# Dividing the softmax exponentials while they are split into halves, in a hybrid pooling and attention layer

## The chip, the cores and the metric

The kernel runs on one core of a Trainium2 chip. Its engines take their instructions each from a queue of its own, in the order in which the program wrote them: TensorE (PE in the profile) for matrix products, VectorE (DVE), ScalarE (ACT), GpSimd (POOL), and SyncE (SP), which here only issues DMA transfers. The metric is the device time of one execution in microseconds (us).

## The reference

One layer on a sequence of 1024 tokens of width 1024, in float32:

```python
h = rmsnorm(x, norm_pre)
pool_u, pool_gate, q, k, v, attn_gate = split(h @ w_in)       # 512, 512, 512, 128, 128, 512 columns
pool_out = pool_mixer(pool_u, pool_w, pool_scale) * silu(pool_gate)
attn_out = swa_sink_attention(q, k, v, sinks) * silu(attn_gate)
y = concat([pool_out, attn_out]) @ w_out
x = x + rmsnorm(y, norm_post)
```

The attention has 8 heads of width 64 that share 2 key and value heads. Queries are taken in blocks of 128; each query sees the 128 keys up to itself, so a block's window lies in its own block of keys and the one before. The scores get a bias that falls with the distance, and each head has a sink, a logit that counts in the softmax's sum and carries no value. The pooling branch takes trailing means over 2, 4, 8 or 16 tokens in four groups of 128 channels, subtracts the token itself, and maps each group by a 128x128 matrix.

## The kernel before

**Halves.** TensorE multiplies fp16 here. Each float32 operand is scaled by a power of two and split into a high and a low fp16 half; a product is three passes (high by high, high by low, low by high; `PASSES`). A split is two instructions: ScalarE writes the high half (`AF.Copy` with a scale), VectorE the low half (value times scale minus high half, `scalar_tensor_tensor`). The power of two comes from a bound on the operand: ScalarE sums absolute values (`abssum`, line 91), TensorE spreads the column over all partitions (`spread`, line 82), VectorE takes its maximum and the power of two (lines 73 to 87).

**Slots.** The input projection is cut in 34 slots. A slot `s` makes 128 columns for 512 tokens (`proj`, line 292): 24 matmuls into one of two PSUM tiles `acc`, emptied by ScalarE in `land_slot`. Slots 0 to 9 are the keys and queries, 10 to 17 the pooling gates, 18 to 25 the pooling inputs (`u`), 26 to 33 the attention gates. Work for other parts hangs between: `middle()` runs after the twelfth matmul of a slot, `early` after the third. From slot 5 on, attention block `n` takes two slots, an even one (s = 5 + 2n, called even in the code since s - 5 is) and an odd one:

- even slot: `score_mm(n)` on TensorE, `score_land(n)` on VectorE (mask by a copy with predicate, bias, maximum of each row as `negm`), `exps(n)` on ScalarE (line 389: eight exponentials of 128x129, one per head, each with its sum)
- odd slot: `turn(n)` and `turn_low(n)` split the exponentials into `ph`; then a DMA on SP's queue transposes `ph` to `full`
- next even slot: `mask(n)` on GpSimd makes from `full` what belongs to the own block (`own`, line 427) and to the block before (`full`, line 431)
- next odd slot, at its end: `pv_mm(n)` multiplies by the values; in the even slot after that `pv_land(n)` puts the result in `cat`

In the program before, the exponentials are split undivided, scaled by 4096. The reciprocals of the sums are laid out by GpSimd to 128x512 (`r`, line 413), turned by four TensorE transposes in `divide(n)` in the middle of the next even slot (`rb`, line 442), put in `cat` by ScalarE with the value scale `vo` (line 443), and `pv_land` multiplies the product by them on VectorE (line 465). `rb` and the product `pvo` share the one buffer of the pool `ps_pv`.

**Pooling.** The landing of a `u` slot (line 476) is taken by `pool_windows` in the slot after (lines 491 to 503); in the middle of the slot after that `pool_mm` multiplies (`mixed`, line 508), and `pool_gate` (line 513) applies the gate. `sums()` in the main loop issues the windows: ahead of the projection before slot 20 (`LATE`), behind it from there. In slots 20 to 23 ScalarE turns the gates in `cat` by Silu (line 798), with one table load in slot 20.

**Output weights.** `w_out` is read twice, in eight tiles `woraw`: once for its bound (`bound_wo`, ScalarE, one tile a slot), once to be split (`split_wo` on ScalarE, `low_wo` on VectorE). `open_late` in slot 22 gives the attention's memory to the split weights.

## Time and profile before

| | us |
|---|---|
| median of 3 runs | 342.42 |
| lowest and highest run | 341.96, 1195.05 |
| the profiled execution, its span | 341.63, 339.9 |
| TensorE busy | 322.6 (95% of the span) |
| VectorE, ScalarE, GpSimd busy | 198.3, 169.6, 66.1 |

The third run, 1195.05, stands far from the other two. A time in a row below is counted from the start of the span of the profiled execution. A row of the timeline begins with the start and the duration, both in us; "idle before" in brackets is how long the engine had stood, and what released it. The span is about 1.7 us shorter than the execution's own time.

### The profile page before, as it was taken

The page shows a single profiled execution, that of the slowest core. Times are in us where ns is not written, and L with a number is a line of the kernel's source. Part 1 is how long each engine was busy: PE and PEld are TensorE (multiplying, and loading weights), DVE is VectorE, ACT ScalarE, POOL GpSimd, SP SyncE. Part 2 cuts the span into 40 slices and gives each one's busy share as a digit, 9 for nine tenths or more (in the row PEclk, how much of TensorE's full clock was granted, in tenths as well). Part 3 has the DMA queues.
Part 4 walks back from the last instruction along what each step waited for, and adds up shares of the span by engine and source line. Part 5 has one row for each costly group of instructions (what it writes and reads, how often), then busy time and mean ns, then how long its engine had stood idle before and what let it go on. Part 6 is the DMA issues. An engine that isn't in the chain of part 4 may idle for free.

```text
span 339.9 us, 5053 instructions
## 1 busy us (share of the span) xinstructions
PE 322.6 (95%) x1913; PEld 166.8 (49%) x1913; DVE 198.3 (58%) x423; ACT 169.6 (50%) x368; POOL 66.1 (19%) x73
## 2 busy tenths in 40 slices
PE   4789999999999999999979999999999999999993
PEld 2688556545445445454434444444444444444442
DVE  4977871537697444796979678833753633310122
ACT  5867831275657675888394573326543442211011
POOL 1101303000142343132405000000000233312330
PEclk9999999999999999999999999999999999999999
DMA  8976240002437376385631690320000341133111
GB/s 279 275 212 189 70 125 0 2 15 49 123 123 183 129 188 152 85 165 117 104 78 46 215 263 20 114 73 0 2 0 0 103 147 67 61 120 123 62 64 62
DMA packets 52090, 35.73 MB, mean 105 GB/s; under 512 B 35041, under 2 KB 45793, under 8 KB 52066
## 3 DMA queue, kind: packets, MB, share of 16 engines
q1 hardware_dynamic: 52064, 35.40, 38.2%
q8 instruction: 15, 0.25, 0.3%
q14 instruction: 9, 0.07, 0.1%
q10 hardware_dynamic: 2, 0.00, 0.0%
HBM read 27.01 MB, written 4.19 MB: 92 GB/s over the span
## 4 chain that ended last, share of the span: by engine, by line
PE 60%; issue 14%; DVE 10%; POOL 8%; ACT 5%; DMA 2%; POOLq 0%; DVEq 0%; ACTq 0%
PE acc L292 41%; POOL o L641 5%; PE pv L272 3%; PE y L272 3%; ACT st L389 3%; PE tp L250 2%; PE sc L360 2%; PE pvo L455 2%; PE mixed L508 2%; PE acc L272 2%; DVE o L638 2%; DMA full<-ph 1%; DVE st L377 1%; PE gain L176 1%; POOL yf L633 1%
## 5 line engine op out<-in xcount | busy, mean ns | idle before, releaser
L292 PE MATMUL acc<-hT,whl 128*128 128x512 f16 x792 | 177.1, 379 | 0.0
L292 PEld LDWEIGHTS <-whl 128*128 128x128 f16 x792 | 76.6, 98 | 91.9 <-issue 6.9
L272 PE MATMUL y<-wo,chl 128*128 128x512 f16 (+2 forms) x408 | 83.6, 366 | 0.0
L272 PEld LDWEIGHTS <-chl 128*128 128x128 f16 x408 | 39.0, 98 | 43.5
L611 ACT ACTIVATE junk<-y 128x512 bf16<-128x512 f32 (+2 forms) x17 | 9.7, 572 | 54.9 <-PE y L272 54.9
L389 ACT ACTIVATE st<-st,negm 128x129 f32<-128x129 f32 x64 | 24.8, 390 | 12.6 <-DVE negm L382 9.5
L613 DVE SCALAR_TENSOR_TENSOR eps_of<-yss,eps_of 128x1 f32<-128x1 f32 x17 | 3.2, 186 | 45.9 <-ACT junk L611 45.9
L219 ACT ACTIVATE whl<-wraw,ws 128x1024 f16<-128x1024 f32 x18 | 20.4, 1145 | 15.9 <-DVE ws L77 12.3
L633 POOL TENSOR_TENSOR yf<-eps_of,mhalf 128x1 f32<-128x1 f32 x7 | 3.8, 549 | 115.1 <-DVE eps_of L613 115.1
L223 DVE SCALAR_TENSOR_TENSOR whl<-wraw,ws,whl 128x1024 f16<-128x1024 f32 x18 | 23.7, 1325 | 0.0
L404 DVE SCALAR_TENSOR_TENSOR ph<-st,ph 128x1024 f16<-128x1024 f32 x8 | 9.8, 1226 | 21.8 <-ACT ph L399 21.8
L641 POOL TENSOR_TENSOR o<-o,xr 128x512 f32<-128x512 f32 x14 | 17.5, 1268 | 9.1 <-DVE o L638 9.1
L91 ACT ACTIVATE whl<-wraw 128x1024 bf16<-128x1024 f32 x18 | 18.8, 1049 | 0.6 <-DMA wraw<-in_w_in_dram 0.6
L427 POOL TENSOR_SCALAR_AFFINE_SELECT own<-full 128x2048 f16<-128x2048 f16 x7 | 14.5, 2072 | 22.9 <-DMA full<-ph 22.9
L413 POOL COPY r<-sums 128x512 f32<-128x512 f32 x8 | 4.9, 610 | 67.8 <-DVE sums L411 45.8
L250 PE MATMUL tp<-ident,h 128*128 128x128 f32 x64 | 11.7, 350 | 5.9 <-DVE h L241 3.4
L95 DVE SCALAR_TENSOR_TENSOR chl<-cat,cs,chl 128x1024 f16<-128x1024 f32 x8 | 10.3, 1285 | 10.2 <-ACT chl L94 10.2
L377 DVE SCALAR_TENSOR_TENSOR st<-sc,qu,bias 128x256 f32<-128x256 f32 x32 | 15.2, 484 | 1.0
L531 ACT ACTIVATE gt<-acc,wu 128x512 f32<-128x512 f32 x8 | 5.5, 687 | 18.9 <-PE acc L292 15.4
L431 POOL TENSOR_SCALAR_AFFINE_SELECT full<-full 128x2048 f16<-128x2048 f16 x7 | 14.4, 2052 | 0.5
L94 ACT ACTIVATE chl<-cat,cs 128x1024 f16<-128x1024 f32 x8 | 9.2, 1147 | 10.0 <-DVE cs L77 10.0
L250 PEld LDWEIGHTS tp<-ident,h 128*128 128x128 f32 x64 | 9.9, 182 | 7.3 <-DVE h L241 3.8
(109 smaller groups left out, 377.0 us busy)
## 6 DMA issues: line engine op xcount, KB each, us to landing
wraw<-in_w_in_dram SPq DMA_DIRECT2D x10, 512.0 KB, 5.1
x<-in_x_dram SPq DMA_DIRECT2D x8, 512.0 KB, 5.2
wraw<-in_w_in_dram SPq DMA_DIRECT2D x16, 256.0 KB, 4.7
woraw<-in_w_out_dram SPq DMA_DIRECT2D x8, 512.0 KB, 5.6
woraw<-in_w_out_dram SPq DMA_DIRECT2D x16, 256.0 KB, 7.0
xr<-in_x_dram SPq DMA_DIRECT2D x8, 512.0 KB, 3.5
out_dram<-o SPq DMA_DIRECT2D x16, 256.0 KB, 2.0
post<-in_norm_post_dram SPq DMA_DIRECT2D x1, 512.0 KB, 4.6
```

The source lines that it names most:

```text
L91: nc.scalar.activation(junk, src, AF.Abs, accum_out=m)
L95: eng.scalar_tensor_tensor(lo, src, s, hi, op0=ALU.mult, op1=ALU.subtract)
L219: nc.scalar.activation(whl[ch][:, 0], raws[ch], AF.Copy, scale=halves[ch])
L223: nc.vector.scalar_tensor_tensor(w[:, 1], raws.pop(ch), s, w[:, 0], op0=ALU.mult, op1=ALU.subtract)
L250: nc.tensor.transpose(flips[tt][b][:, block_of(i)], h[:, block_of(4 * b + i)], ident)
L272: nc.tensor.matmul(acc, a, b, start=i == 0, stop=i == len(pairs) - 1)
L292: nc.tensor.matmul(acc, w[:, a, k, :], hT[:, b, k, half_of(half)], start=k == 0 and i == 0, stop=k == KT - 1 and i == 2,)
L377: nc.vector.scalar_tensor_tensor(st[:, hs, :P], sc[:, :, 0 if n else 1, :], qu[:, 2 * pr : 2 * pr + 1], (bias if n else bias0)[:, hs, :], ...
L389: nc.scalar.activation(st[:, h, :], st[:, h, :], AF.Exp, bias=negm[:, h : h + 1], accum_out=sums[:, h : h + 1],)
L427: nc.gpsimd.affine_select(o, f, pattern=[[0, 16], [1, P]], compare_op=ALU.is_ge, fill=0.0, base=0, channel_multiplier=-1,)
L431: nc.gpsimd.affine_select(f, f, pattern=[[0, 16], [-1, P]], compare_op=ALU.is_ge, fill=0.0, base=-1, channel_multiplier=1,)
L641: nc.gpsimd.tensor_tensor(o[:, hs], o[:, hs], xr[:, hs], op=ALU.add)
```

## The change

The reciprocal of each sum, times 4096, is made ahead of the split (`turn`), and the split takes it as its scale: eight 128x128 instructions on ScalarE and eight on VectorE, a pair for each head, in place of one 128x1024 instruction on each. The layout on GpSimd, the transposes on TensorE and `divide` go. `pv_land` becomes a copy with the value scale on ScalarE, in place of a product on VectorE. In the main loop `turn` stands behind `sums()` and `lows()` before slot 20, and in slot 20 behind the Silu and ahead of the projection. The bounds of the output weights go from slots 11 to 18 to slots 17 to 24 (`WO`), their loads with them, and the second loads and the high halves come two slots later; the last low halves come two in a slot where two are ready.

```diff
     def turn(n):
         st, sums = att_s.pop(n)
         ph = att.tile([P, 2, 8, P], F16, tag="ph", name="ph")
-        nc.scalar.activation(ph[:, 0], st[:, :, :P], AF.Copy, scale=4096.0)
+        nc.vector.tensor_scalar(sums, sums, 2.0**-12, None, op0=ALU.mult)
+        nc.vector.reciprocal(sums, sums)
+        for h in range(8):
+            nc.scalar.activation(
+                ph[:, 0, h], st[:, h, :P], AF.Copy, scale=sums[:, h : h + 1]
+            )
         att_f[n] = (st, sums, ph)
 
     def turn_low(n):
         st, sums, ph = att_f[n]
-        nc.vector.scalar_tensor_tensor(
-            ph[:, 1], st[:, :, :P], 4096.0, ph[:, 0], op0=ALU.mult, op1=ALU.subtract
-        )
+        for h in range(8):
+            nc.vector.scalar_tensor_tensor(
+                ph[:, 1, h], st[:, h, :P], sums[:, h : h + 1], ph[:, 0, h],
+                op0=ALU.mult, op1=ALU.subtract,
+            )
...
-        nc.vector.reciprocal(sums, sums)
-        r = t2.tile([P, 512], F32, tag="t2", name="r")
-        nc.gpsimd.tensor_copy(
-            r.rearrange("p (c kv d) -> p c kv d", c=4, kv=2),
-            sums.rearrange("p (kv c) -> p c kv", kv=2).unsqueeze(3).broadcast_to([P, 4, 2, HD]),
-        )
...
-    def divide(n):
-        r = att_r.pop(n)
-        rb = ps_pv.tile([P, 512], F32, tag="pv", name="rb")
-        for c in range(4):
-            nc.tensor.transpose(rb[:, block_of(c)], r[:, block_of(c)], ident)
-        nc.scalar.activation(
-            cat[:, 4:8, block_of(n)], rb.rearrange("p (c t) -> p c t", t=P), AF.Copy, scale=vo
-        )
...
     def pv_land(n):
-        dst, pv = cat[:, 4:8, block_of(n)], att_o.pop(n)
-        nc.vector.tensor_tensor(dst, pv.rearrange("p (c t) -> p c t", t=P), dst, op=ALU.mult)
+        nc.scalar.activation(
+            cat[:, 4:8, block_of(n)], att_o.pop(n).rearrange("p (c t) -> p c t", t=P),
+            AF.Copy, scale=vo,
+        )
...
+        WO = 17
...
-            elif n < NB:
-                turn(n)
...
-                if not odd and 1 <= n <= NB:
-                    divide(n - 1)
...
+            if odd and n < NB and s >= LATE:
+                turn(n)
             if s < LATE:
                 sums()
                 lows()
+                if odd and n < NB:
+                    turn(n)
                 acc = proj(ch, half, middle)
...
-                if s >= 26 and wo_lo < wo_hi:
-                    low_wo(wo_lo)
-                    wo_lo += 1
+                for _ in range(2 if s >= 31 else 1):
+                    if wo_lo < wo_hi:
+                        low_wo(wo_lo)
+                        wo_lo += 1
...
-            if 9 <= s < 9 + KT:
-                wo_raw["b", s - 9] = load_wo(s - 9)
-            if 11 <= s < 11 + KT:
-                bound_wo(s - 11)
-            if s == 11 + KT:
+            if WO - 2 <= s < WO - 2 + KT:
+                wo_raw["b", s - WO + 2] = load_wo(s - WO + 2)
+            if WO <= s < WO + KT:
+                bound_wo(s - WO)
+            if s == WO + KT - 1:
...
-            if s >= 23 and wo_hi < KT:
+            if s >= 25 and wo_hi < KT:
...
-            if 21 <= s < 21 + KT:
-                wo_raw["o", s - 21] = load_wo(s - 21)
+            if WO + KT - 2 <= s < WO + 2 * KT - 2:
+                wo_raw["o", s - WO - KT + 2] = load_wo(s - WO - KT + 2)
```

VectorE before, in block 1, from the low half of an input weight (L223) past the power of two of the next weights (L87 to L213) to the split of the exponentials (L404), the landing of a query slot (L95) and `pv_land` (L465):

```order
L223 SCALAR_TENSOR_TENSOR whl<-wraw,ws,whl 128x1024
L87 TENSOR_REDUCE amall<-spread 128x1
L73 TENSOR_SCALAR wp<-amall 128x1
L76 TENSOR_SCALAR wp<-wp 128x1
L77 RECIPROCAL ws<-wp 128x1
L213 TENSOR_TENSOR wu<-wp,gsc 128x1
L404 SCALAR_TENSOR_TENSOR ph<-st,ph 128x1024
L411 RECIPROCAL sums<-sums 128x8
L95 SCALAR_TENSOR_TENSOR qT<-acc,qT 128x512
L465 TENSOR_TENSOR cat<-pvo,cat 128x4x128
```

The same place of the changed kernel:

```order
L223 SCALAR_TENSOR_TENSOR whl<-wraw,ws,whl 128x1024
L399 TENSOR_SCALAR sums<-sums 128x8
L400 RECIPROCAL sums<-sums 128x8
L87 TENSOR_REDUCE amall<-spread 128x1
L73 TENSOR_SCALAR wp<-amall 128x1
L76 TENSOR_SCALAR wp<-wp 128x1
L77 RECIPROCAL ws<-wp 128x1
L213 TENSOR_TENSOR wu<-wp,gsc 128x1
L410 SCALAR_TENSOR_TENSOR ph<-st,sums,ph 128x128 x8
L95 SCALAR_TENSOR_TENSOR qT<-acc,qT 128x512
```

The reciprocals, which need the sums of all exponentials, now stand ahead of the power of two; `pv_land` is gone from the engine.

VectorE before, in slot 20, from the windows of the second pooling slot (L491 to L503, `u` slot 19) over the split of block 7 to the gate of the first:

```order
L491 TENSOR_TENSOR win<-ug 128x527
L491 TENSOR_TENSOR win<-win 128x525
L497 SCALAR_TENSOR_TENSOR res<-win,ug 128x512
L502 TENSOR_TENSOR win<-win,invc 128x3
L503 TENSOR_TENSOR res<-win,ug 128x3
L404 SCALAR_TENSOR_TENSOR ph<-st,ph 128x1024
L411 RECIPROCAL sums<-sums 128x8
L513 SCALAR_TENSOR_TENSOR cat<-mixed,pscale,cat 128x512
```

The same place of the changed kernel:

```order
L399 TENSOR_SCALAR sums<-sums 128x8
L400 RECIPROCAL sums<-sums 128x8
L483 TENSOR_TENSOR win<-ug 128x527
L483 TENSOR_TENSOR win<-win 128x525
L489 SCALAR_TENSOR_TENSOR res<-win,ug 128x512
L494 TENSOR_TENSOR win<-win,invc 128x3
L495 TENSOR_TENSOR res<-win,ug 128x3
L410 SCALAR_TENSOR_TENSOR ph<-st,sums,ph 128x128 x8
L505 SCALAR_TENSOR_TENSOR cat<-mixed,pscale,cat 128x512
```

The reciprocals of block 7 have come ahead of these windows.

ScalarE before, from the exponentials of block 7 (L389) to the next landings; L798 is the Silu of a gate, L476 and L481 land `u`:

```order
L389 ACTIVATE st,sums<-st,negm 128x129 x8
L399 ACTIVATE ph<-st 128x1024
L798 ACT_TABLE_LOAD
L798 ACTIVATE cat<-cat 128x1024
L476 ACTIVATE ug<-acc,wu 128x512
L481 ACTIVATE tails<-acc,wu 128x16
```

The same place of the changed kernel:

```order
L389 ACTIVATE st,sums<-st,negm 128x129 x8
L790 ACT_TABLE_LOAD
L790 ACTIVATE cat<-cat 128x1024
L402 ACTIVATE ph<-st,sums 128x128 x8
L91 ACTIVATE junk,wom<-woraw 128x1024
L468 ACTIVATE ug<-acc,wu 128x512
L473 ACTIVATE tails<-acc,wu 128x16
```

The split of block 7 now stands behind the table load and the first Silu, and the bound of an output weight tile ahead of the landing.

## Rows read from the trace of the kernel before

**Rows 1.** The page's busy times: us, share of the span, instructions.

```profile
PE 322.6 (95%) x1913; PEld 166.8 (49%) x1913; DVE 198.3 (58%) x423; ACT 169.6 (50%) x368; POOL 66.1 (19%) x73
```

**Rows 2.** Timeline of TensorE around the first three `divide`.

```profile
77.75 0.27 PE L82 MATMUL spread<-ident,as 128*128 128x128 f32 x1
77.86 0.60 PE L442 MATMUL rb<-ident,r 128*128 128x128 f32 x4
78.30 5.34 PE L292 MATMUL acc<-hT,whl 128*128 128x512 f16 x24
...
91.05 0.27 PE L82 MATMUL spread<-ident,as 128*128 128x128 f32 x1
...
92.55 5.34 PE L292 MATMUL acc<-hT,whl 128*128 128x512 f16 x24
...
103.35 2.76 PE L292 MATMUL acc<-hT,whl 128*128 128x512 f16 x12
...
106.80 7.93 PE L292 MATMUL acc<-hT,whl 128*128 128x512 f16 x36
```

**Rows 3.** Groups by line: count, busy us, mean ns, idle before.

```profile
L389 ACT ACTIVATE st<-st,negm 128x129 f32<-128x129 f32 x64 | 24.8, 390 | 12.6 <-DVE negm L382 9.5 <-POOL full L431 3.0
...
L404 DVE SCALAR_TENSOR_TENSOR ph<-st,ph 128x1024 f16<-128x1024 f32 x8 | 9.8, 1226 | 21.8 <-ACT ph L399 21.8
...
L399 ACT ACTIVATE ph<-st 128x1024 f16<-128x1024 f32 x8 | 8.5, 1057 | 0.3
...
L465 DVE TENSOR_TENSOR cat<-pvo,cat 128x512 f32<-128x512 f32 x8 | 5.3, 665 | 0.3 <-PE pvo L455 0.3
...
L613 DVE SCALAR_TENSOR_TENSOR eps_of<-yss,eps_of 128x1 f32<-128x1 f32 x17 | 3.2, 186 | 45.9 <-ACT junk L611 45.9
...
L411 DVE RECIPROCAL sums<-sums 128x8 f32<-128x8 f32 x8 | 1.6, 196 | 0.0
```

**Rows 4.** Timeline of all engines, from block 1's masks to block 2's product.

```profile
93.82 1.24 DVE L213 TENSOR_TENSOR wu<-wp,gsc 128x1 f32<-128x1 f32 x1
...
94.99 0.16 DVE L371 COPY st<-sinks 128x8 f32<-128x8 f32 x1
...
99.85 0.41 ACT L389 ACTIVATE st<-st,negm 128x129 f32<-128x129 f32 x1 [3.71 <-DVE negm L382]
...
105.46 1.65 SPq L408 DMA_TRANSPOSE full<-ph  x1
...
109.24 2.00 POOL L427 TENSOR_SCALAR_AFFINE_SELECT own<-full 128x2048 f16<-128x2048 f16 x1 [2.99 <-DMA full<-ph]
...
114.66 0.84 PE L455 MATMUL pvo<-own,vst 128*64 128x512 f16 x6
115.33 0.81 PE L455 MATMUL pvo<-full,vst 128*64 128x512 f16 x6
```

**Rows 5.** Timeline of all engines in slots 20 and 21, block 7.

```profile
168.83 0.41 ACT L389 ACTIVATE st<-st,negm 128x129 f32<-128x129 f32 x1 [3.02 <-POOL full L431]
...
169.44 0.71 DVE L491 TENSOR_TENSOR win<-ug 128x527 f32<-128x527 f32 x1
...
171.85 0.16 DVE L503 TENSOR_TENSOR res<-win,ug 128x3 f32<-128x3 f32 x1
...
172.42 2.76 PE L292 MATMUL acc<-hT,whl 128*128 128x512 f16 x12
173.13 1.28 ACT L798 ACT_TABLE_LOAD   x1
...
175.39 0.67 ACT L476 ACTIVATE ug<-acc,wu 128x512 f32<-128x512 f32 x1
...
177.49 1.02 PE L508 MATMUL mixed<-res,pw 128*128 128x512 f32 x2
```

**Rows 6.** The same timeline, where GpSimd's mask of block 7 meets VectorE.

```profile
178.36 2.48 POOL L427 TENSOR_SCALAR_AFFINE_SELECT own<-full 128x2048 f16<-128x2048 f16 x1 [3.11 <-DMA full<-ph]
...
179.01 2.37 DVE L497 SCALAR_TENSOR_TENSOR res<-win,ug 128x512 f32<-128x512 f32 x1
```

More of the change, by code (lines that the diff above doesn't have):

```diff
@@ L410, in turn_low @@
         )
-        nc.vector.reciprocal(sums, sums)
-        r = t2.tile([P, 512], F32, tag="t2", name="r")
-        nc.gpsimd.tensor_copy(
-            r.rearrange("p (c kv d) -> p c kv d", c=4, kv=2),
-            sums.rearrange("p (kv c) -> p c kv", kv=2).unsqueeze(3).broadcast_to([P, 4, 2, HD]),
-        )
         att_f[n] = full
-        att_r[n] = r
     def mask(n):
```

## The prediction

> **What bounds the kernel now.** The page's busy times come first: TensorE is busy 95% of the span, the others 58% and less [rows 1]. So an edit is worth what it takes off TensorE's own queue or out of its waits, and costs what it makes TensorE wait for. The timeline of TensorE around `divide` is read next, by starts, since ends of matmuls overlap. Twelve more matmuls in a burst take 7.93 - 5.34 = 2.59 us, 0.216 each [rows 2]. The first `divide` holds the queue for 78.30 - 77.86 = 0.44. The second, from the `spread` ahead of it, takes 92.55 - 91.05 = 1.50, against 78.30 - 77.75 = 0.55 at the first: 0.95 more, waiting for the shared buffer, so 1.39. The third takes 106.80 - 103.35 - 2.59 = 0.86. The last, in slot 21, takes 177.49 - 172.42 - 2.59 = 2.48 [rows 5]. The four between show no wait: 0.44 each. Last I followed one attention block through all engines, since TensorE meets its result two slots later: block 2 [rows 4] and block 7 [rows 5].
>
> **What is removed.** 0.44 + 1.39 + 0.86 + 4 x 0.44 + 2.48 = 6.9 us of TensorE's queue. This is the most that the change can give, 2.0% of the profiled 341.63. GpSimd loses eight layouts and VectorE eight `pv_land`, 0.67 each [rows 3]; ScalarE's copy in `pv_land` replaces that in `divide`, of the same size.
>
> **What is added to a block's chain.** From the first exponential to the DMA's issue the kernel before takes 5.61 in block 2 (99.85 to 105.46) [rows 4]. Out of it go one ScalarE copy, 1.06, and one VectorE low half, 1.23 [rows 3]. In come:
> - two small VectorE instructions on 128x8, 0.2 each by the reciprocal's row, and one more change of engine, estimated at 0.1: 0.5.
> - eight 128x128 ScalarE copies with a scale from memory. No such row exists. Lower end: an eighth of the large copy, 0.13 each, 1.06 in all; upper end: the exponential of a head, nearly the same shape and with a pointer too, 0.39 each, 3.1 in all [rows 3]. ScalarE's neighbours overlap: a table load at 173.13 of 1.28 and a Silu of the large copy's size, 1.06, would end at 175.47, and the next starts at 175.39 [rows 5]. So 8 x (0.39 - 0.08) + 0.08 = 2.5, near the upper end, because its row has the same shape.
> - eight VectorE low halves. Each runs one head behind ScalarE, so only the last counts. Between a one-column instruction, 0.186, and the large one, 1.226, in proportion to width: 0.32 [rows 3].
>
> Sum: 0.5 + 2.5 + 0.32 - 1.06 - 1.23 = +1.0 a block; the ends give -0.4 and, with no overlap of the two engines (2.6), about +3.9.
>
> **Blocks 1 and 2.** ScalarE's queue behind block 1's split (a weight's high half, a bound, the landing of a query slot) moves 0.5 + 1.44 = 1.9 later, and VectorE's low half of that landing with it. Without `pv_land` VectorE gets 0.67 back. Whether it also gets back 1.05 at L213, which took 1.24 beside GpSimd's mask where a one-column instruction takes 0.19, is open [rows 3, 4]. So `score_land(2)`, at 94.99 before, starts 0.2 to 1.2 later, and the DMA of block 2, 1.0 more, 1.2 to 2.2 later: 106.7 to 107.7. From issue to the own mask it takes 109.24 - 105.46 = 3.78, and a mask 2.0 [rows 4]. The own mask ends at 112.4 to 113.4, the other one at 114.5 to 115.5. TensorE, freed of three divides (2.69), comes to the product at 114.66 - 2.69 = 111.97 and waits for both. Its second half starts at 114.5 to 115.5; it was 115.33 [rows 4]. Of 2.7 us gained to there some 0.3 is left: **the loss is 2.4**. A stall here gives later blocks time; I see no further wait in blocks 3 to 6, whose four divides bring 1.76. TensorE leads by 2.1.
>
> **Block 7.** TensorE would end the first half of slot 21 at 172.42 + 2.59 - 2.1 = 172.9, and then wants the windows of the second `u` slot (`mixed`). Before, VectorE made them from 169.44 to 172.01, beside the exponentials of block 7, and had them done early [rows 5]. Now the reciprocals stand ahead of them and wait for all eight exponentials: queued behind are these windows, behind them TensorE. Block 6's exponentials can start some 0.7 to 1.2 earlier by the lead there, its split pushes the `u` landing behind it 1.9 later; the windows before `score_land(7)`, and so block 7's exponentials, come 0.7 to 1.2 later: 169.5 to 170.0 instead of 168.83. Eight of them take 3.1, the reciprocals 0.5, the windows 2.57: 175.7 to 176.2. **TensorE waits 3.0** and starts `mixed` at 176.0 instead of 177.49: lead 1.5. Slot 22 needs the accumulator of slot 20 back. ScalarE now has, from the exponentials' end at 172.9, table load 1.28, Silu 1.06, split 2.5, a weight bound of the moved series about 1.06 (a 1024-wide row), landing 0.9: 179.7. TensorE would be there at 176.0 + 0.86 + 2.59 = 179.45: a wait of 0.25. The third `u` slot's windows, one longer by 0.71, need 3.3 from that landing, 179.4: 182.7, against TensorE's 182.3: 0.4 more. The lead at the end is 0.8. Block 7's masks are done before its product.
>
> ScalarE's page in the Trainium skill ("ScalarE: Activation LUTs", What ACT_TABLE_LOAD costs) puts a drain of 1.38 us on every table switch besides the load. The trace disagrees: between 173.13 and 175.39 there is room for load and Silu alone [rows 5]. By the page the split of block 7 and the landing would come 1.4 later, and the sum would be a gain of nothing instead of 0.8.
>
> **The moved bounds.** Eight ScalarE instructions leave slots 11 to 18 and come in slots 17 to 24, where each stands ahead of a landing; that is in the sum above. Their loads now share SP's queue with the transposes of blocks 5 to 7: the order on the queue puts loads behind a transpose that waits for a split, with two slots between load and use as cover (over 10 us; without it ScalarE, and the landing behind, would stand). The high halves of `w_out` end two slots later, hidden since the last low half stays in slot 33, where it was. The column's `spread` only moves. Priced at nothing.
>
> **Forecast.** 6.9 - 2.4 - 3.0 - 0.25 - 0.4 = 0.8 (rounded), so 340.8 for an execution like the profiled one. That one lies 0.3 and 0.8 below the other two undisturbed runs (341.96, 342.42); their middle is 342.0, and I predict 341.2.
>
> **Rivals.**
> - *The heads are cheap.* If a ScalarE head costs nearer to 0.13 than 0.31, block 2's mask is there before TensorE, and block 7's chain starts earlier: about 2 us come back at block 2 and 1 to 1.5 at block 7, a gain of 4: 338.0. For it speaks the large copy's rate, against it the exponential's row. If the windows' wait vanished too, all 6.9 would stay: 335.1.
> - *VectorE and GpSimd collide: slower than before.* In block 7 the row of `res` takes 2.37 beside GpSimd's own mask, which runs from 178.36 for 2.48 [rows 6]; the rate of the line in row 169.44 (0.71 for about the same width) says what it takes alone. Now the masks start 3.78 after an issue near 178.1, at 181.9, and the third windows end at 182.7: the mask would catch their last instructions, which read two tiles. Then `mixed` waits up to 2.2 more, and the next mask may take another 1 to 2 from the windows of the fourth slot: 0.8 becomes a loss of 1.4 to 3.4, 343.4 to 345.4. It decides from the point at which these windows are unfinished when the mask begins. For it: the times lie within 1 us. Against: an instruction that has begun holds on, and a slightly shorter split puts the windows ahead.
> - *The drain* of the page, which the row denies: 342.0.
>
> The Trainium skill's "SBUF — State Buffer" (Who interferes with whom) has a VectorE instruction with two SBUF inputs and a GpSimd one that reads SBUF block each other fully. By that rule the collision is all or nothing; the row at 179.01 agrees, with its 2.37.
>
> **How the numbers follow.** Forecast 0.5 (339.7 to 342.5); cheap heads 0.22 (335.1 to 339.7); collision 0.22 (342.5 to 345.4); drain 0.03; the upper end of the chain at every block, above 345.4, 0.03. The range that leaves out 0.1 on each side goes from 337.8 into the cheap heads to 344.0 into the collision. About 2% either way, 6.8 us, is what a measurement can tell from no change. Faster by more than that takes all of the 6.9: 0.04. Slower by more takes +3.9 at each block: 0.03. Within: 0.93.
>
> **What the changed profile would show.** No L442 row; eight ScalarE copies a block of about 0.39, 0.31 apart; TensorE waiting for the masks of block 2 (L445) and for `mixed` in slot 21, released by VectorE; VectorE idle ahead of L399, released by the exponentials. Wrong would be: no wait at block 2, copies closer than 0.2, or TensorE standing at other landings than slot 20's.

## The result and the profile after

The changed kernel takes 345.46 us (median of seven executions, 344.12 to 347.05), against 342.5 for the kernel before: 1.0089 times as long, interval [1.0071, 1.0107]. The forecast was 341.2 (337.8 to 344.0). It missed: the change costs 3 us where I expected a gain of about 1.

The page's busy times, for [rows 1], come first, then the groups by line that the change made (columns as in [rows 3]).

```profile
PE 322.2 (94%) x1881; PEld 164.4 (48%) x1881; DVE 203.8 (59%) x479; ACT 179.7 (52%) x424; POOL 61.3 (18%) x65
```

```profile
L402 ACT ACTIVATE ph<-st,sums 128x128 f16<-128x128 f32 x64 | 19.5, 387 | 3.7 <-ACT st L389 3.2 <-DVE sums L400 0.5
L410 DVE SCALAR_TENSOR_TENSOR ph<-st,sums,ph 128x128 f16<-128x128 f32 x64 | 18.3, 348 | 1.6 <-ACT ph L402 1.6
...
L371 DVE COPY st<-sinks 128x8 f32<-128x8 f32 x8 | 3.2, 394 | 0.0
L400 DVE RECIPROCAL sums<-sums 128x8 f32<-128x8 f32 x8 | 1.6, 203 | 0.3
L399 DVE TENSOR_SCALAR sums<-sums 128x8 f32<-128x8 f32 x8 | 1.4, 172 | 18.7 <-ACT st L389 18.7
```

ScalarE has 10 us more and VectorE 5.5. A ScalarE head takes 0.387, a low half 0.348. L371, the copy of the sinks into a block's tile of scores, is an old instruction; its mean of 394 ns for 128x8 is the odd figure here.

TensorE's timeline in slots 11 and 12, block 2:

```profile
103.09 5.34 PE L292 MATMUL acc<-hT,whl 128*128 128x512 f16 x24
110.30 5.34 PE L292 MATMUL acc<-hT,whl 128*128 128x512 f16 x24 [1.87 <-ACT cat L518]
115.57 0.84 PE L445 MATMUL pvo<-own,vst 128*64 128x512 f16 x6
117.11 0.84 PE L445 MATMUL pvo<-full,vst 128*64 128x512 f16 x6 [0.71 <-POOL full L431]
```

ScalarE's timeline there:

```profile
106.19 2.44 ACT L402 ACTIVATE ph<-st,sums 128x128 f16<-128x128 f32 x8 [0.53 <-ACT st L389]
...
109.58 0.67 ACT L518 ACTIVATE cat<-acc,wu 128x512 f32<-128x512 f32 x1
```

Slot 12 could start at 103.09 + 24 x 0.216 = 108.27 and starts at 110.30: its accumulator is held until ScalarE lands slot 10 (L518), which stands behind the exponentials of block 2 and its eight heads. Then 0.87 is lost to a mask. Before, [rows 2] (36 matmuls in a row from 106.80) and [rows 4] show no wait there.

Block 7, in four engines' timelines; [rows 5] are its counterpart:

```profile
163.58 0.67 ACT L468 ACTIVATE ug<-acc,wu 128x512 f32<-128x512 f32 x1
...
166.84 2.32 POOL L427 TENSOR_SCALAR_AFFINE_SELECT own<-full 128x2048 f16<-128x2048 f16 x1 [11.02 <-DMA full<-ph]
167.22 1.98 DVE L371 COPY st<-sinks 128x8 f32<-128x8 f32 x1
169.10 0.42 DVE L376 COPY_PREDICATED sc<-own_key,sc 128x256 f32<-128x256 uint16 x1
169.23 2.00 POOL L431 TENSOR_SCALAR_AFFINE_SELECT full<-full 128x2048 f16<-128x2048 f16 x1
169.55 0.48 DVE L377 SCALAR_TENSOR_TENSOR st<-sc,qu,bias 128x256 f32<-128x256 f32 x1
...
170.14 1.10 PE L500 MATMUL mixed<-res,pw 128*128 128x512 f32 x2 [2.56 <-issue]
171.07 4.44 PE L292 MATMUL acc<-hT,whl 128*128 128x512 f16 x12
...
173.90 0.40 ACT L389 ACTIVATE st<-st,negm 128x129 f32<-128x129 f32 x1 [7.14 <-DVE ug L472]
...
177.11 1.28 ACT L790 ACT_TABLE_LOAD   x1
177.12 0.17 DVE L399 TENSOR_SCALAR sums<-sums 128x8 f32<-128x8 f32 x1 [3.23 <-ACT st L389]
...
178.40 1.06 ACT L790 ACTIVATE cat<-cat 128x1024 f32<-128x1024 f32 x1
179.37 2.42 ACT L402 ACTIVATE ph<-st,sums 128x128 f16<-128x128 f32 x8
...
180.11 1.10 PE L500 MATMUL mixed<-res,pw 128*128 128x512 f32 x2 [0.49 <-DVE res L495]
```

The product of the first `u` slot (u0, the `mixed` of slot 20) starts 2.7 us after TensorE could have started it. The page can't name what held it ("issue"). Its windows were done at 166.10; what it lacks is a PSUM bank: all four of that pool hold the scores of block 7. The first is free when L377 ends, 169.55 + 0.48 = 170.03, and the product starts at 170.14. The score landing was late because its first instruction, the copy of the sinks, took 1.98 instead of 0.17 beside GpSimd's mask of block 6. Behind the standing TensorE the clock falls. Windows of the trace (engines' busy times, then PEclk, DMA share, GB/s):

```profile
168.00:170.00 2.00, 0.00 (x0) 0.00 (x0) 1.97 (x4) 0.00 (x0) 1.93 (x2) 1.00 0.71 162
170.00:172.00 2.00, 1.86 (x5) 0.78 (x6) 1.93 (x6) 0.00 (x0) 1.24 (x1) 0.82 1.22 247
172.00:174.00 2.00, 2.00 (x6) 0.76 (x5) 1.82 (x4) 0.10 (x1) 0.00 (x0) 0.50 0.54 123
174.00:176.00 2.00, 2.00 (x12) 0.71 (x11) 0.00 (x0) 2.00 (x11) 0.00 (x0) 0.82 0.00 0
```

Granted 0.50, the lower of the two levels (1.2 GHz), makes twelve matmuls (171.07) take 4.37 to the next start instead of 2.6. So TensorE first stands and then runs slowly in this stretch; what the second costs is asked by k9 below.

One more such place lies ahead of the change: in the profiled execution the clock was 0.50 from 18 to 24 us too, in code that is the same in both kernels, and TensorE reached the first scores at 62.85 instead of 61.45. Therefore I compare profiles by stretches from that point on: to the scores of block 7 (slot 19), from there to the product of u1 (the `mixed` of slot 21), and from there to the first product of the output. All are differences of starts on TensorE's timeline (before: 61.45, 157.72, 177.49, 250.62; after: 62.85, 158.22, 180.11, 254.68). By their sum the change costs 2.66 us; the 1.40 ahead of the first scores is left out.

| kernel | time (median), us | the profiled execution | to scores 7 | to product u1 | to output | sum |
|---|---|---|---|---|---|---|
| before | 342.5 | 341.63 | 96.27 | 19.77 | 73.13 | 189.17 |
| after | 345.46 | 345.69 | 95.37 | 21.89 | 74.57 | 191.83 |
| k3_undivided | 339.97 | 340.34 | 93.05 | 16.98 | 76.41 | 186.44 |
| k7_recip_only | 340.2 | 340.15 | 93.06 | 19.55 | 73.99 | 186.60 |
| k6_heads_only | 345.46 | 344.99 | 95.41 | 19.88 | 77.46 | 192.75 |
| k10_low_heads | 339.83 | 340.00 | 93.45 | 17.74 | 75.15 | 186.34 |
| k11_high_heads | 342.73 | 345.18 | 96.22 | 18.91 | 76.42 | 191.55 |
| k8_sinks_first | 343.09 | 341.85 | 95.26 | 19.82 | 74.57 | 189.65 |
| k9_filler | 345.98 | 346.26 | 95.31 | 21.89 | 75.52 | 192.72 |
| k17_block6_whole | 343.29 | 343.10 | 95.29 | 20.24 | 74.58 | 190.11 |
| k19_vector_heads | 344.06 | 344.04 | 95.15 | 20.21 | 76.00 | 191.36 |

A wait that is taken away in one column often comes back in the next; so a verdict goes by the time, and the columns only say where. They belong to the profiled execution, which in k8 and k11 lies far from the median. The kernel before took 341.9 to 342.6 (medians) beside the runs below.

### The profile page after: what moved, and what is told of

Same layout as the page of the kernel before. It is cut to its first block, busy times and chain, and to the rows that moved or that the text cites. A ratio compares the mean times of both kernels' runs of the same rounds, so it can differ in the third digit from the quotient of the medians.

```text
span 344.0 us, 5077 instructions
## 1 busy us (share of the span) xinstructions
PE 322.2 (94%) x1881; PEld 164.4 (48%) x1881; DVE 203.8 (59%) x479; ACT 179.7 (52%) x424; POOL 61.3 (18%) x65
## 5 line engine op out<-in xcount | busy, mean ns | idle before, releaser
L389 ACT ACTIVATE st<-st,negm 128x129 f32<-128x129 f32 x64 | 24.8, 390 | 23.8 <-DVE negm L382 16.7
L219 ACT ACTIVATE whl<-wraw,ws 128x1024 f16<-128x1024 f32 x18 | 20.4, 1147 | 10.1 <-DVE ws L77 5.5
L223 DVE SCALAR_TENSOR_TENSOR whl<-wraw,ws,whl 128x1024 f16<-128x1024 f32 x18 | 23.4, 1312 | 1.4 <-ACT whl L219 1.4
L402 ACT ACTIVATE ph<-st,sums 128x128 f16<-128x128 f32 x64 | 19.5, 387 | 3.7 <-ACT st L389 3.2
L410 DVE SCALAR_TENSOR_TENSOR ph<-st,sums,ph 128x128 f16<-128x128 f32 x64 | 18.3, 348 | 1.6 <-ACT ph L402 1.6
L95 DVE SCALAR_TENSOR_TENSOR chl<-cat,cs,chl 128x1024 f16<-128x1024 f32 x8 | 10.3, 1284 | 10.2 <-ACT chl L94 10.2
L250 PE MATMUL tp<-ident,h 128*128 128x128 f32 x64 | 10.9, 332 | 5.6 <-DVE h L241 3.4
L377 DVE SCALAR_TENSOR_TENSOR st<-sc,qu,bias 128x256 f32<-128x256 f32 x32 | 15.2, 484 | 1.0
L250 PEld LDWEIGHTS tp<-ident,h 128*128 128x128 f32 x64 | 9.1, 172 | 6.9 <-DVE h L241 3.8
```

Source lines behind the costliest of these rows:

```text
L219: nc.scalar.activation(whl[ch][:, 0], raws[ch], AF.Copy, scale=halves[ch])
L223: nc.vector.scalar_tensor_tensor(w[:, 1], raws.pop(ch), s, w[:, 0], op0=ALU.mult, op1=ALU.subtract)
L250: nc.tensor.transpose(flips[tt][b][:, block_of(i)], h[:, block_of(4 * b + i)], ident)
L377: nc.vector.scalar_tensor_tensor(st[:, hs, :P], sc[:, :, 0 if n else 1, :], qu[:, 2 * pr : 2 * pr + 1], (bias if n else bias0)[:, hs, :], ...
L389: nc.scalar.activation(st[:, h, :], st[:, h, :], AF.Exp, bias=negm[:, h : h + 1], accum_out=sums[:, h : h + 1],)
L402: nc.scalar.activation(ph[:, 0, h], st[:, h, :P], AF.Copy, scale=sums[:, h : h + 1])
```

## The experiments

**Moved bounds or division?** k1 takes the change and puts the bounds of the output weights back six slots; k2 takes the kernel before and moves them.

```
k1, on the kernel after      k2, on the kernel before: the reverse
-        WO = 17
+        WO = 11
-            if s >= 25 and wo_hi < KT:
+            if s >= 23 and wo_hi < KT:
...
```

k1: 

> The changed kernel with the bounds of the output weights back in slots 11 to 18. Theory one (the chain): the split head by head and the reciprocals delay VectorE's landing of the scores, on which TensorE's banks, masks and windows hang, so the 2.7 us wait ahead of the first mixed product stays and the time is 344 to 347. Theory two (the moved bounds): the bound instructions that now stand ahead of the landings on ScalarE and their loads make the waits of slots 20 to 22, so these vanish and the time is 340 to 341.5.

k2: 

> The kernel before with only the bounds of the output weights moved to slots 17 to 24. Theory one: 342.5 to 343.5, at most the 0.6 us that the moved spread costs in slot 25. Theory two: 345 or more, with TensorE waiting in slots 20 to 22.

Measured: k1 347.07, ratio 1.0125 [1.0095, 1.0155]; k2 343.2, 1.0034 [1.0019, 1.0048]. The moved bounds alone cost 0.8 to 1.2 us (difference of the times, ratio), mostly where the weights' overall bound is spread in slot 25 (in k2, from the product in slot 24 to that in slot 25, 6.85 us instead of 6.14; 6.85 in the changed kernel too). But in the changed kernel moving them is worth 1.6. Put back, the spread of the bound stands in slot 20 ahead of the product of u0 and takes 1.74 of the wait there; then VectorE makes the bound's power of two ahead of the windows of u1, and TensorE waits longer for those:

```profile
180.63 2.04 PE L500 MATMUL mixed<-res,pw 128*128 128x512 f32 x2 [2.94 <-DVE res L495]
```

Behind that wait the granted clock is 0.71 and 0.72 (178 to 182 and 182 to 190 us). So the move is not where the loss comes from; the theory that it is falls.

**Without the division.** k3 splits in one instruction per step by 4096 and makes no reciprocals. k4 keeps the change and lands the scores at the head of every even slot, ahead of windows and low halves.

```
k3
-        nc.vector.tensor_scalar(sums, sums, 2.0**-12, None, op0=ALU.mult)
-        nc.vector.reciprocal(sums, sums)
-        for h in range(8):
-            nc.scalar.activation(ph[:, 0, h], st[:, h, :P], AF.Copy, scale=sums[:, h : h + 1])
+        nc.scalar.activation(ph[:, 0], st[:, :, :P], AF.Copy, scale=4096.0)
 (the low halves likewise)
k4
+            if not odd and n < NB:
+                score_land(n)
             if s < LATE:
                 sums()
                 lows()
```

k3: 

> The changed kernel with the split as one ScalarE and one VectorE instruction with the constant 4096, and no reciprocals: the division by the sums is left out. Theory one: without the long split the waits at block 2 and in slots 20 to 22 go and the 6.9 us of the divides stay, 335.5 to 337.5. Theory two: the waits of slots 20 to 22 stay, 341 or more.

k4: 

> The changed kernel with the landing of the scores on VectorE ahead of the pooling windows and the low weight halves of its slot. Theory one: the chain gets 2 to 5 us back in each block, the bank for the first mixed product is free in time, 336 to 339. Theory two: ScalarE is as late as before, 344 or more.

Measured: k3 339.97, 0.9931 [0.9908, 0.9953]; k4 352.33, 1.0286 [1.0254, 1.0318]. k3 lies between its two theories; k4 lies in the range of the second, though not for its reason. The division in heads costs 5.5 us (345.46 to 339.97), but without any division TensorE still gains only 2.4 of the 6.9 taken off its queue: it then meets a mask (0.56), a landing (0.85), windows (0.93) and the moved spread in slot 25 (0.7); the rest is in smaller pieces that I did not assign. In k4 TensorE waits 5.2 more in slots 9 and 10 (1.69 for VectorE's landing of a query slot, 3.53 for a spread), and the windows of u0, put off, run into both masks of block 6, so that it waits 4.78 for their product:

```profile
171.51 2.42 DVE L483 TENSOR_TENSOR win<-ug 128x527 f32<-128x527 f32 x1
173.97 2.37 DVE L489 SCALAR_TENSOR_TENSOR res<-win,ug 128x512 f32<-128x512 f32 x1
```

**Heads or reciprocals?** k6 keeps both rows of heads, by a constant column, and makes no reciprocals; k7 makes the reciprocals, unread, and splits whole.

```
k6  -  scale=sums[:, h : h + 1]   (and the same in turn_low)
    +  scale=even[:, h : h + 1]      # a column of 4096
k7  the reciprocals stay, both split steps as in k3
```

k6: 

> The changed kernel with the eight heads of both split steps kept, but multiplied by a constant column of 4096 and not by the reciprocals, which are not made: the division by the sums is left out. VectorE then has no instruction that stands until the exponentials are done; ScalarE and VectorE still do their eight heads (2.44 and 2.21 us). Taking the whole division out was worth 5.5 us (345.5 to 340.0). Theory one (the longer split on ScalarE and VectorE costs it: the landing behind it comes 1.4 us later, the masks 1 us later): 343.5 to 345.5, most of the 5.5 stays. Rival, theory three (the reciprocals cost it, because VectorE stands at them until ScalarE has done the exponentials, up to 3.2 us, and the windows and landings queued behind come late): 340 to 341.5, with the wait for the windows of u1 and u2 and the late landing of block 7 gone.

k7: 

> The changed kernel with the reciprocals made at the same place, their result read by nobody, and each split step one instruction by 4096 as it was before the change: the division by the sums is left out. VectorE still stands at the reciprocals until the exponentials are done; the split itself is short. Theory one (the longer split costs it): 340 to 341.5, like the kernel without any division. Theory three (VectorE's standing costs it): 343.5 to 345.5, with the product of u0 still waiting for the scores of block 7 to be landed and the clock falling behind it.

Measured: k6 345.46, 1.0097 [1.0082, 1.0112]; k7 340.2, 0.9948 [0.9931, 0.9965]. The heads carry the whole price, VectorE's standing at the reciprocals next to nothing. That standing was the largest wait of the forecast. In k7 the wait is there, but not its price: the stretch to the product of u1 is 19.55 instead of k3's 16.98, and the next one gives it back, 73.99 instead of 76.41.

```profile
175.14 1.10 PE L495 MATMUL mixed<-res,pw 128*128 128x512 f32 x2 [2.17 <-DVE res L490]
```

**Which engine's heads?** k10 leaves only VectorE's low halves in heads, k11 only ScalarE's high ones (by the constant column; the other step as in k3, reciprocals unread).

k10: 

> The changed kernel with the first split step (ScalarE) one instruction by 4096 again and only the second (VectorE) in eight heads, by a constant column of 4096; the reciprocals are made and read by nobody: the division by the sums is left out. Two heads of cost were taken together so far (5.3 to 5.5 us). Per block the two forms stand to each other so: both steps whole 1.06 + 1.23 = 2.29 us one behind the other, both in heads 2.44 + 0.35 = 2.79, this one 1.06 + 2.21 = 3.27. Theory ScalarE (its 1.38 us more per block hold up the landings queued behind): 340 to 341.5. Theory chain (what counts is when the second step ends, since the transposing transfer and the masks follow): this form is the longer one, 345.5 to 347. Theory VectorE (its 0.98 us more per block): 343.5 to 345.5.

k11: 

> The counterpart: the first split step (ScalarE) in eight heads by a constant column of 4096, the second (VectorE) one instruction by 4096; the reciprocals are made and read by nobody: the division by the sums is left out. Per block 2.44 + 1.23 = 3.67 us one behind the other. Theory ScalarE: 344.5 to 346, nearly all of the 5.5 us. Theory chain: 346 to 348, the longest form of all. Theory VectorE: 340 to 341.5.

Measured: k10 339.83, 0.9940 [0.9925, 0.9955]; k11 342.73, 1.0041 [1.0017, 1.0064]. VectorE's heads and a later end of the split cost nothing in sum: k10's chain, from the first exponential of block 2 to the issue of its transfer, is as long as the changed kernel's (6.67 and 6.61 us; 5.60 in k3). ScalarE's heads cost 2.9 us, not all; the 2.7 from k11 to the changed kernel belong to a collision, the next experiment. It is absent from k10 and present in k3, so that a cost of the longer chain and a gain there may cancel. Of k11's ten executions seven took 342.4 to 342.9 and three, the profiled one among them, 345.2 to 345.6; in its profile the granted clock fell behind 2.1 us of waiting for block 2's masks (0.79 on the mean from 114 to 122 us). The seven have a higher mean clock over the whole (0.989 to 0.993, against 0.977 to 0.982); that this fall is what they lack is likely, and not shown, since none of them was profiled. ScalarE's timeline shows the mechanism, first in k10, then in k11:

```profile
155.86 1.06 ACT L403 ACTIVATE ph<-st 128x1024 f16<-128x1024 f32 x1
...
159.13 0.67 ACT L467 ACTIVATE ug<-acc,wu 128x512 f32<-128x512 f32 x1
```

```profile
158.62 2.43 ACT L404 ACTIVATE ph<-st,even 128x128 f16<-128x128 f32 x8
...
163.03 0.67 ACT L468 ACTIVATE ug<-acc,wu 128x512 f32<-128x512 f32 x1
```

From the start of the split to the landing of u0 behind it: 3.27 and 4.41 us. The windows of u0 and the scores of block 7 follow from that landing, on VectorE.

**The collision.** k8 issues the copy of the sinks at the head of the slot, ahead of windows and low halves, all else as in the changed kernel.

```
+            if not odd and n < NB:
+                score_open(n)        # the tile and the copy of the sinks
             if s < LATE:
                 sums()
```

> The changed kernel with the copy of the sinks into the tile of scores (128x8, 1.98 us in block 7 of the changed kernel where it meets GpSimd's mask of block 6, 0.17 elsewhere) issued at the head of the slot, before the windows and the low halves of the weights; everything else stays. Theory of the collision: the landing of block 7 starts some 1.8 us earlier, the product of u0 waits about 0.9 instead of 2.74 for its bank, the granted clock doesn't fall behind it, and 341.5 to 343 is left of 345.5. Rival: the copy only took the blow for whatever VectorE does next beside that mask, the next copy or add is held in its place, and the time stays at 344.5 to 346.

Measured: 343.09, 1.0039 [1.0018, 1.0060]. The copy takes 0.16, the product of u0 starts 2.2 us earlier (105.10 after the first scores, against 107.29), and in the profiled execution, the fastest of the ten, no clock falls there; the wait for u1 is then there in full:

```profile
166.30 1.10 PE L505 MATMUL mixed<-res,pw 128*128 128x512 f32 x2 [0.48 <-PE acc L292]
...
176.28 1.10 PE L505 MATMUL mixed<-res,pw 128*128 128x512 f32 x2 [2.17 <-DVE res L500]
```

That is 2.4 us for one copy of 128x8 in this kernel. In the profile of k11 the copy comes 0.16 ahead of the mask and misses it (166.67 and 166.83). The instruction behind it isn't held in its place: in k8 the landing runs beside the same mask at its usual 0.42 and 0.49.

The heads don't bring copy and mask together: in k3 and k7, which split whole, the copy takes 1.98 and 1.97 too. GpSimd's and VectorE's timelines of k3:

```profile
161.81 2.40 POOL L420 TENSOR_SCALAR_AFFINE_SELECT own<-full 128x2048 f16<-128x2048 f16 x1 [8.96 <-DMA full<-ph]
162.26 1.98 DVE L371 COPY st<-sinks 128x8 f32<-128x8 f32 x1
```

There the product of u0 waits some 0.2 us all the same; whether the exponentials of block 7, later by it, cost something further on no run isolates. Where ScalarE's queue is held longer, the meeting costs 2.4 (k8 to the changed kernel) and 2.2 (k15 to k14 below).

**The clock.** k9 fills the standing ahead of the product of u0 with twelve matmuls whose result nobody reads.

```
+                if s == 20:
+                    fill = ps_sp.tile([P, 512], F32, tag="sp", name="fill")
+                    for _ in range(12):
+                        nc.tensor.matmul(fill, whl[ch][:, 0, 0, :], hT[:, 0, 0, half_of(half)], start=True, stop=True)
```

> The changed kernel with twelve matmuls of 512 columns, whose result is read by nobody, put into TensorE's queue right ahead of the product of u0 in slot 20, where TensorE stood 2.74 us for a bank before its granted clock fell to half. They need some 2.6 us, so that the wait is filled and no later matmul starts later than it did. Theory of the clock (the fall follows from the standing, and costs 1.78 us in the slot's second half): granted clock 1.00 in the 8 us behind, the second half of the slot 2.7 to 2.9 us long instead of 4.44, and 343 to 344.5. Rival (the clock falls for another reason, or the 1.78 us are given back at the next wait, for the windows of u1): 345 to 346.

Measured: 345.98, 1.0112 [1.0095, 1.0128]: the rival.

```profile
167.05 2.75 PE L824 MATMUL fill<-hT,whl 128*128 128x512 f16 x12
169.77 1.10 PE L500 MATMUL mixed<-res,pw 128*128 128x512 f32 x2
170.71 2.75 PE L292 MATMUL acc<-hT,whl 128*128 128x512 f16 x12
...
179.74 1.10 PE L500 MATMUL mixed<-res,pw 128*128 128x512 f32 x2 [2.17 <-DVE res L495]
```

The clock stayed at 1.00 from 170 to 176 us and the 1.78 us were back, but TensorE then stood 2.17 at u1's windows, behind which the clock fell (0.74 from 178 to 184). The table has the same 21.89 in both. The slow clock of the changed kernel was thus paid in time that VectorE's chain (scores of block 7, exponentials, reciprocals, windows of u1) would have taken anyway.

**Other orders on top of k8.** k12 puts the windows of u1 ahead of the reciprocals in slot 20; k13 besides makes the reciprocals in two halves of four heads and puts the bound of an output weight behind the slot's landing.

```
k12          if odd and n < NB and s >= LATE:
+                sums()
                 turn(n)
```

k12: 

> The version with the sinks copied first (343.1), and besides the windows of u1 issued ahead of the reciprocals in slot 20, the one slot in which they stand behind them. There VectorE had stood 3.23 us for the exponentials of block 7 and TensorE 2.17 us for the windows behind. Theory (VectorE's standing is that wait): the product of u1 no longer waits, and 341 to 342 is left if nothing later takes it. Rival (given back: the windows of u2 wait for their landing on ScalarE, whose exponentials, table load, gate and eight heads fill 170 to 178 us whatever VectorE does): the product of u2 waits as much longer, and 342.7 to 343.5 stays.

k13: 

> The version with the sinks copied first and the windows of u1 ahead of the reciprocals, and two more orders: the reciprocals of heads 0 to 3 made while the exponentials of heads 4 to 7 still run, so that ScalarE's first head needn't wait its 0.52 us; and from slot 17 on the landing of a slot ahead of the bound of an output weight on ScalarE (1.23 us). Theory (each was a wait on the path): block 2 loses 0.5 us less, the windows of u2 start 1.2 us earlier, 340.5 to 341.8, below the kernel before (342.3). Rival (the masks of block 2 and the landing of u2 stay late for other reasons): 342.3 to 343.5.

Measured: k12 342.6, 1.0031 [1.0007, 1.0056]; k13 343.07, 1.0033 [1.0020, 1.0046]. Both rivals, in the main: in k12 u1 waits no longer, and slot 22 waits for ScalarE's landing of slot 20 instead, as long as k8 had stood at u1:

```profile
PE acc L292 <- ACT tails L478: 2.2, 1, 2.2
```

In k13 (94.86, 16.79, 78.12) the first two stretches gain 0.4 and 0.7 over k12 (95.27, 17.48, 76.92), and the last loses 1.2: in slot 25 TensorE waits 1.6 instead of 0.4 ahead of the spread of the output weights' bound.

**One block alone.** k17 splits block 6 whole (as in k3), the other seven in heads.

> The changed kernel with only block 6's two split steps in one instruction each by 4096 (for that block the division by the sums is left out), the other seven blocks in heads. If the time that the heads cost comes from ScalarE's queue in slot 18, where the eight heads of block 6 stand ahead of the landing of u0, so that its windows, the score landing of block 7 behind them and all that follows come late: the landing of u0 1.4 us earlier, the copy of the sinks at least partly clear of the mask, the product of u0 waiting at most 1 us instead of 2.74, and 342 to 344 of 345.5. Rival (block 7's own heads, and block 2's, carry the cost): 344.7 to 346.

Measured: 343.29, 1.0035 [1.0007, 1.0062]; the time is as expected. The landing of u0 comes 1.7 us earlier (99.0 after the first scores instead of 100.7), the product of u0 waits 0.90, though the sinks' copy still meets the mask (1.97). Two of the 5.5 us hang on block 6's split alone.

**The division elsewhere.** k14 divides the block's exponentials in place by one VectorE product and splits whole; k15 adds the order of k8, k16 that and the old place of the bounds; k18 puts the first step's heads on GpSimd, k19 both rows of heads on VectorE.

```
k14 +  nc.vector.tensor_tensor(st[:, :, :P], st[:, :, :P],
    +      sums.unsqueeze(2).to_broadcast([P, 8, P]), op=ALU.mult)
    ...  (both split steps as in k3)
k18 -  nc.scalar.activation(ph[:, 0, h], st[:, h, :P], AF.Copy, scale=sums[:, h : h + 1])
    +  nc.gpsimd.tensor_scalar(ph[:, 0, h], st[:, h, :P], sums[:, h : h + 1], None, op0=ALU.mult)
k19    the same with nc.vector, in turn_low
```

k14: 

> The changed kernel with the whole division kept but done by VectorE: one product of the block's exponentials with the reciprocals, broadcast along each head (128x1024, estimated at 1.25 us from the low half of that size, 1.23), and then both split steps in one instruction each by 4096. ScalarE has its 1.06 us per block back; the chain from the exponentials to the end of the split is 0.2 + 1.25 + 1.06 + 1.23 = 3.74 us, longer than the 0.5 + 2.79 = 3.3 of the changed kernel. Theory ScalarE (its 1.38 us per block are the cost): 339.5 to 341.5, below the kernel before (342.0 to 342.4). Rival chain (the end of the split counts) or VectorE (its busy time counts, 0.5 us more per block than in heads): 344.5 to 347.

k15: 

> The division on VectorE as one product, and the copy of the sinks issued at the head of the slot. Theory ScalarE: with the landing of u0 early again, the score landing of block 7 may start ahead of GpSimd's mask of block 6 anyway, so that the order of that copy brings 0 to 1.8 us more: 338.5 to 341. Rival: as the run without it within 0.5 us.

k16: 

> The same, and the bounds of the output weights back in slots 11 to 18. In the kernel before the moved bounds cost 0.8 to 1.0 us, in the changed kernel, whose ScalarE was the late engine, they saved 1.6. Theory ScalarE: with 1.38 us per block given back to ScalarE, the bounds are as in the kernel before and their return brings 0 to 0.8: 338 to 340.5. Rival: they stand ahead of the landings of blocks 2 and 3 still, and cost 0.5 to 1.5: 340.5 to 342.

k18: 

> The changed kernel, division complete, with the eight heads of the first split step on GpSimd instead of ScalarE (VectorE's eight heads stay). ScalarE has nothing left of the split: from its last exponential on it goes to the landings at once, where in the changed kernel it stood 0.5 us and worked 2.44, and in the version with the division as one product on VectorE it stood 1.58 and worked 1.06, 2.97 against 2.64 us, which is why that one, in hindsight, gained nothing. Theory ScalarE's queue (what counts is how long the landings wait behind the split on ScalarE, standing included): no wait of TensorE for a landing at slot 12, the landing of u0 2 us earlier, 338.5 to 341.5, below the kernel before (342.3). Rival collision: GpSimd's heads and VectorE's low halves, masks and windows hold each other up, the heads take 0.5 us and more each, and the masks of blocks 2 and 7 come 2 us later: 344 to 348.

k19: 

> The changed kernel, division complete, with the eight heads of both split steps on VectorE, the first ones ahead of the second ones. ScalarE has nothing of the split, VectorE 8 x 0.28 = 2.2 us more per block, and the end of the split, and so the masks, come 2 us later than in the changed kernel. Theory ScalarE's queue: TensorE meets the masks of block 2 about 2 us later but no late landing, 340 to 344; block 7 no later than in the run with heads on VectorE alone. Rival chain (the end of the split counts in every block): 346 to 350, with waits for own and full in blocks 2 to 7.

Measured: k14 346.26, 1.0122 [1.0081, 1.0164]; k15 344.05, 1.0050 [1.0034, 1.0066]; k16 344.91, 1.0076 [1.0052, 1.0099]; k18 350.3, 1.0235 [1.0194, 1.0275]; k19 344.06, 1.0050 [1.0035, 1.0065]. k14 lies in its rival's range, k15 and k16 in neither of theirs, k18 above both, k19 at the upper end of its theory's. ScalarE's timeline of k14 says why: after the last exponential it stands 1.58 us until VectorE has divided, and the landing of u0 comes as late as with heads.

```profile
158.12 0.18 ACT L389 ACTIVATION_READ_ACCUMULATOR st<-st,negm 128x1 f32 x1
159.88 1.06 ACT L403 ACTIVATE ph<-st 128x1024 f16<-128x1024 f32 x1 [1.58 <-issue]
...
162.93 0.67 ACT L465 ACTIVATE ug<-acc,wu 128x512 f32<-128x512 f32 x1
```

That fits a queue on ScalarE that counts as long as it is held, standing included. k19, which takes the split off ScalarE, is 1.4 us below the changed kernel, but its copy of the sinks misses the mask (0.17, at 165.94, the mask at 166.79), as in k8, and against k8 it is 1.0 slower, though the landing of u0 comes 0.7 earlier (99.7 after the first scores instead of 100.4): TensorE waits for block 2's masks (0.86 and 1.24), 2.17 for the windows of u1 and 1.49 for those of u2. So it doesn't show by itself what a free ScalarE queue is worth. In k18 GpSimd's eight heads take 4.68 where ScalarE's took 2.44, and VectorE's low halves can only follow them one by one:

```profile
105.52 4.68 POOL L402 TENSOR_SCALAR ph<-st,sums 128x128 f16<-128x128 f32 x8 [3.28 <-DVE amall L87]
```

```profile
106.16 4.42 DVE L410 SCALAR_TENSOR_TENSOR ph<-st,sums,ph 128x128 f16<-128x128 f32 x8
```

VectorE's eight took 2.2 behind ScalarE. GpSimd's first head, with no low half beside it, takes 0.60 like the later ones, so the heads are slow on GpSimd itself; only in block 7, where VectorE's windows of u1 run beside them, do the eight take 5.53. No version that divides came out below the kernel before; k12 is nearest, at 1.0031.

## Why the prediction was wrong

- *What is removed*: right. To the third block TensorE gained 0.44 and 1.38, read from [rows 2] as 0.44 and 1.39 (between the starts of the second, third and fourth score products: 13.31 and 14.90 before, 12.87 and 13.52 after). But k3, with nothing added to the chain, keeps only 2.4 of the 6.9: most of what is removed doesn't come out as time even then.
- *What is added to a chain*: right in size. Eight ScalarE heads take 2.44 (forecast 2.5), the last low half comes one head behind, 0.35 (0.32); the small instructions 0.17 and 0.20. From the first exponential to the DMA's issue block 2 takes 6.61 (102.47 to 109.08) instead of 5.61, the +1.0 of the sum. The choice of the exponential's row over the large copy's was the good one. The rival of cheap heads was out.
- *Block 2*: forecast a loss of 2.4, measured 2.03 + 0.87 = 2.9, but from two waits, the larger for a landing behind ScalarE's heads. I had priced a later mask only. TensorE at another landing than slot 20's was one of the signs of being wrong. The 1.05 at L213, left open, didn't come back: it took 1.18 beside the mask again.
- *Block 7, the step that failed* (with a smaller part in the moved bounds). I let block 6's exponentials start 0.7 to 1.2 earlier by TensorE's lead, and so block 7's exponentials only 0.7 to 1.2 later, at 169.5 to 170.0. Measured, with the 1.40 of the start taken off, block 6's start 0.16 later than before (155.43 - 1.40, against 153.87), block 7's at 172.50 and the product of u1 at 178.71, where I had 176.0. That is 2.7 us, and 1.8 of it is the sinks' copy beside the mask. The 0.9 left is the lead that didn't arrive: at the scores of block 6 TensorE led by 0.47 (81.85 after the first scores, against 82.32), and VectorE's landing of them not at all, since a weight's low half ahead of it waited for ScalarE's high half, which stands behind the heads of block 5 (L219 at 147.35, L223 at 148.52).
- *The rival of a collision* had the right mechanism in the wrong place. I put it at the windows of u2 beside block 7's mask, with the landings ahead of it seen as clear; it came at the score landing beside block 6's mask. It isn't the heads that bring it there, since k3 and k7 have the same meeting. That its range, 343.4 to 345.4, almost held the result is partly luck: the result also has the missing lead and the moved bounds in it.
- *The moved bounds*, priced at nothing: 0.7 at slot 25 in the profile, 0.8 to 1.2 by k2 (though in the changed kernel putting them back costs 1.6, by k1). With u2's wait (0.68, forecast 0.25 + 0.4), the last stretch loses 1.44 instead of 0.65.
- *The account*: 2.7 + 0.8 = 3.5 us more than forecast; the forecast had TensorE reach the output 0.8 earlier, it reaches it 2.66 later (189.17 against 191.83). By the times it is 4.3 more (345.46 against 341.2); 0.5 of that is the kernel before, which I took at 342.0 and whose median is 342.5, and some 0.3 is not assigned.
- *The drain*: none. The table load at 177.11 ends at 178.39, the Silu starts at 178.40.

By the runs: ScalarE's heads cost 2.9 us (k10 to k11) to 3.3 (k10 to k8), between kernels whose chains are about as long (6.67, 6.85 and 6.61 in block 2) and whose copy of the sinks is clear of the mask. With these heads the copy in the mask's way costs 2.4 more (k8 to the changed kernel). The two come near the 5.5 from k3, but k3 has the copy in the mask's way as well: they are prices in this order, not parts of one sum. What is shown is the price of each. That all of the first goes through the landings, and not through the masks of block 2 as well, is argued from k17 (2.2 by block 6 alone); k19 speaks for the masks where they come later still. The split between the two blocks stays open.

## What to carry to other kernels

Taking work off the busiest engine is worth only what the next engine's results allow: follow what is queued behind a lengthened instruction on its own in-order queue, landings above all, standing time included. A lead of the busy engine doesn't move the others earlier unless they wait for it. Where two engines can hold each other up, look for every small instruction that a shift of 1 to 2 us brings under the other's long one, and ask what PSUM bank or accumulator it then keeps, and whether the busy engine gets there in that time: with the same 1.98 us of copy TensorE stood 2.7 us in the changed kernel and 0.2 in k3.

## What the runs showed of the hardware

- A VectorE copy of 128x8 from SBUF to SBUF took 1.98 us when issued 0.4 us after GpSimd's mask began (0.17 in the other blocks), and the mask 2.32 instead of 2.00; both ended within 0.05 us of each other. The copies and products on PSUM scores behind it ran beside the second mask at their usual 0.42 and 0.48. The Trainium skill, "SBUF — State Buffer" (Who interferes with whom), says that a plain VectorE copy can, when its operands meet the mode's conditions, enter a mode that takes the ports shared with GpSimd and that an instruction with at most one SBUF input outside such modes doesn't contend; the rows agree, though none names the mode that the copy ran in.
- GpSimd's heads of 128x128 took 0.60 us each (4.68 for eight), with and without a low half on VectorE beside them (k18, block 2). VectorE's low halves behind them took 0.45 each instead of 0.35.
- A ScalarE copy of 128x128 with a scale from memory took 387 ns, eight in a row 2.44. The Trainium skill, "ScalarE: Activation LUTs" (What ACT_TABLE_LOAD costs), gives 186 ns + 0.833 per column, 93 for a pointer operand and 93 of overlap: by it an estimated 386 and 2.44; the trace agrees. The drain of 1.38 us in the same section isn't in this trace.
- A stand of TensorE of 2 to 3 us was followed by the lower clock level for several us in the changed kernel (2.74 ahead of the product of u0, then granted 0.50) and in k9 (2.17 at u1, 0.74 from 178 to 184), but not in k8 (2.17 at u1, granted clock 1.00 in the stretch behind it) nor k6 (2.88 at u0, 1.00).
